# First four key strips by rows of k, the first memory tile alone, and products that nobody reads

## The chip, the core and the metric

One Trainium2 chip, of which this kernel uses one core. The metric is device time in microseconds (us) of one execution. The kernel before takes 1377.06 us, the median of three runs (1375.69 to 1378.71). A core has five engines with a queue of instructions each, worked off in order: TensorE (PE in the profile; its weight loads are PEld), VectorE (DVE), ScalarE (ACT), GpSimd (POOL) and SyncE (SP, which only issues transfers). A wait at the head of a queue holds back all that stands behind it.

## The reference, cut

One layer of an encoder for 256 prompt tokens and 32 sample tokens (288 columns together), width 2048:

```python
h = rmsnorm(x, norm_in)
(a_q, a_k, a_v, i_q, i_k, i_w, a_z, b_z, b_xbc, b_dt, m_q, m_z, gates) = split_cols(h @ w_in)
mkv = rmsnorm(mem_prompt, norm_mem[l]) @ w_mem_kv[l]
mk_p = mkv[..., :M_WIDTH].reshape(bp, N_MEM, M_HEADS, M_HEAD_DIM)
mv_p = mkv[..., M_WIDTH:].reshape(bp, N_MEM, M_HEADS, M_HEAD_DIM)
...
merged = g_a * (ya @ w_pa) + g_b * (yb @ w_pb) + g_m * (ym @ w_pm)
return x + merged @ w_o, (k_new, v_new, i_k, conv_state, h_last)
```

The change is about `mk_p`, the keys of the memory: 256 memory tokens of width 2048, normed, times 2048 x 1024 weights. It is the first thing that the kernel computes.

## The kernel before, in words

All weights (some 200 MB) are streamed once. A weight tile is 512 KB: for a product with 2048 inputs it holds half a strip, that is 128 output channels and 8 of the 16 rows of k (a row of k is 128 inputs). Every weight tile goes through `convert`: SP loads it into `wr`, ACT makes `wh` (a rounded copy in the fast float format), DVE makes `wl` (the rest, `wr - wh`), and PE multiplies. The moving operand is split likewise into a high and a low part, so a row of k is three products: wh with high, wh with low, wl with high. `wr`, `wh` and `wl` have three buffers each.

`jobs` holds the tiles in their order. `run` pops one, calls `convert` for a later one, emits the products (`go`) and then calls `step`, which hands out one piece of side work from the generators that are active, at most two at a time. A generator that yields n comes back n tiles later. `hook` puts a plain function between two tiles. Two `convert` calls stand ahead of `run`, so the third weight tile is converted in the first round.

At the start (lines 70 to 365) the memory is loaded in four tiles of four rows of k (`memraw`, tag A), which ACT and DVE split into `memh` (B) and `meml` (C), with the gain of the norm multiplied in. The norm's root is only needed afterwards, since it is a factor per token. For it, `mem_squares` squares the memory on POOL, two instructions of two rows each in one step, and DVE adds the squares up in `macc` one step later, with a last fold of the two halves. `mem_rstd` lets PE sum `macc` over the partitions (a product with `ones`) and makes the root; `ev_mk` calls it once, when strip 4 is done, scales the four strips that wait in `mkT` (E), and scales the later ones as they come. `x_norm` is the same for the input x (D): eight loads on POOL's queue, squares on ACT, sums on POOL (`ev`), a product with `ones`, and then the split into xh and xl. It must be done when `begin_x` is reached, after all memory products.

The first three strips of keys take the first halves first and the second halves after them; the other five go half after half; then come two blocks of memory values (`mv_block`, 8 tiles each).

Of the kernel before, what the change touches and what calls it, by code (L numbers as in the profile page):

```python
# [7 lines left out]
F32 = mybir.dt.float32  # L8
# [5 lines left out]
P = 128  # L14
# [9 lines left out]

# column blocks of the combined projection, in the order in which the kernel walks them
N_MQ, N_IQ, N_AK, N_AV, N_AQ, N_MZ, N_XBC, N_G = 8, 8, 2, 2, 8, 8, 24, 16
# [7 lines left out]
def step_kernel(ctx, tc, ins, outs):  # L34
# [32 lines left out]
    def mm(out, lhsT, rhs, start=True, stop=True):  # L67
        PE.matmul(out, lhsT, rhs, start=start, stop=stop)  # L68

    # ------------------------------------------------------------------ loads of the start  # L70
    N = Names()
# [8 lines left out]
    S.preload_act_table_set("natural_log_exp_and_others")  # L80
    nc.sync.dma_start(N.memraw[:, 0:4], ins["memT"][:, 0:4])
    cols = const.tile([P, 272], F32, name="cols")
    S.dma_start(cols, ins["cols"])
    g_mem, g_in, g_ssm, g_fin, d_col = (cols[:, 16 * i:16 * i + 16] for i in range(5))
    cw = cols[:, 80:176].rearrange("p (c i) -> p c i", c=24)
# [6 lines left out]
    G.memset(ones, 1.0)  # L92
    ident = const.tile([P, P], F32, name="ident")
    G.affine_select(ident, ones, pattern=[[1, P]], compare_op=OP.is_equal, fill=0.0, base=0,
                    channel_multiplier=-1)
# [3 lines left out]

    # ------------------------------------------------------------------ norms  # L100
    def rsqrt(v, p, n, size):
        """v = 1/sqrt(p / size + EPS), [128, n]; p in PSUM."""
        r, u = t2(n), t2(n)
        S.activation(r, p, AF.Ln, scale=1.0 / size, bias=eps)  # L104
        V.tensor_scalar(v, p, 1.0 / size, EPS, OP.mult, OP.add)
        S.activation(r, r, AF.Exp, scale=-0.5)
        V.scalar_tensor_tensor(u, r, -0.5, r, OP.mult, OP.mult)
        V.tensor_tensor(u, u, v, OP.mult)
        V.scalar_tensor_tensor(v, u, 1.5, r, OP.add, OP.mult)
# [14 lines left out]

    # ------------------------------------------------------------------ the streamed products
    jobs = []          # halves: (dram ap, shape, matmul emitter)
    conv = []          # converted halves that wait for their products
    state = {"c": 0}

    def strip(halves, mov, evac, n=T):  # L130
        """One block of 128 output channels; halves of its weights [128, 8, 128]."""
        box = {}
        for j, ap in enumerate(halves):
            def go(wh, wl, j=j):
                hi, lo = getattr(N, mov) if isinstance(mov, str) else mov
                if j == 0:
                    box["p"] = ps()
                p = box["p"][:, 0:n]
                k0 = 8 * j
                last = j == len(halves) - 1  # L140
                for i in range(8):
                    mm(p, wh[:, i], hi[:, k0 + i], j == 0 and i == 0, False)
                    mm(p, wh[:, i], lo[:, k0 + i], False, False)
                for i in range(8):
                    mm(p, wl[:, i], hi[:, k0 + i], False, last and i == 7)
                if last:
                    evac(p)
            jobs.append((ap, [P, 8, P], go))
# [20 lines left out]
    def hook(f):  # L169
        """f is called between the products before and after it."""  # L170
        jobs.append((None, None, f))

    def convert():
        i = state["c"]
        if i >= len(jobs):
            return
        state["c"] += 1
        ap, shape, go = jobs[i]
        if ap is None:
            conv.append((None, None, go))  # L180
            return convert()
        raw = wpool.tile(shape, F32, tag="wr", name="wr")
        nc.sync.dma_start(raw, ap)
        wh = wpool.tile(shape, F32R, tag="wh", name="wh")
        wl = wpool.tile(shape, F32R, tag="wl", name="wl")
        S.activation(wh, raw, AF.Copy)  # L186
        V.tensor_tensor(wl, raw, wh.bitcast(F32), OP.subtract)  # L187
        conv.append((wh, wl, go))

    # ------------------------------------------------------------------ side work  # L190
    queue, active = [], []
# [8 lines left out]
    def turn(key, gap):  # L200
        """Waits until gap halves have passed since the turn before this one."""
        while clock["t"] < clock.get(key, 0):
# [4 lines left out]
    def later(*fs):  # L207
        """Each of fs one half further on than the one before it."""
        chains.append(list(fs))
# [44 lines left out]

    # ------------------------------------------------------------------ memory keys and values
    N.mkT = slot("E", [P, 8, 256])
# [3 lines left out]

    def mem_load(k0):
        nc.sync.dma_start(N.memraw[:, k0:k0 + 4], ins["memT"][:, k0:k0 + 4])

    def mem_split(k0):
        for k in range(k0, k0 + 4):
            g = g_mem[:, k:k + 1]
# [3 lines left out]

    def mem_squares():
        N.macc = t2()
        sq = []
# [22 lines left out]
    def ev_mk(s):  # L296
        def f(p):
            if s < 4:
                S.activation(N.mkT[:, s], p, AF.Copy)
                return  # L300
            if s == 4:
                mem_rstd()
                V.tensor_tensor(N.mkT[:, 0:4], N.mkT[:, 0:4],
                                N.mr[:, None, 0:256].to_broadcast([P, 4, 256]), OP.mult)
                G.dma_start(outs["mem_k"][:, 0:4], N.mkT[:, 0:4])
            V.tensor_tensor(N.mkT[:, s], p, N.mr[:, 0:256], OP.mult)
            if s == 7:
                G.dma_start(outs["mem_k"][:, 4:8], N.mkT[:, 4:8])
        return f

    def ev_mv(c):
# [5 lines left out]

    def x_norm():
        acc = ev()
        for k in range(0, 16, 2):  # L320
# [22 lines left out]

    for s in range(3):
        strip([ins["w_mk"][s, h] for h in range(2)], (N.memh, N.meml), ev_mk(s), 256)
    jobs[:] = jobs[0::2] + jobs[1::2]
    jobs.insert(1, (None, None, lambda: mem_split(12)))
    for s in range(3, 8):
        strip([ins["w_mk"][s, h] for h in range(2)], (N.memh, N.meml), ev_mk(s), 256)
    for c in range(2):  # L350
        mv_block(c, ev_mv(c))

    mem_split(0)
    convert()
    mem_load(4)
    mem_split(4)
    convert()
    mem_load(8)
    mem_load(12)
    mem_split(8)  # L360
    dts = const.tile([P, 64], F32, name="dts")
# [4 lines left out]

    # ------------------------------------------------------------------ projections of the step
    wi = {"s": 0}
# [40 lines left out]

    # ---- memory attention  # L410

    def softmax(p, c, width_, scale):
        """Rows of p [128, c * width_]: c softmaxes; the maximum is subtracted."""
        m = st()
# [74 lines left out]

    # ---- index keys, index weights, step sizes  # L490
    wt = const.tile([P, 3, 64], F32, name="wt")
# [13 lines left out]

    # columns of dts: step sizes, their products with -exp(a_log), running sums
    dt = const.tile([P, 96], F32, name="dt")
# [5 lines left out]
    def g_misc():  # L513
# [13 lines left out]
        mark("misc")  # L527
        # log(1 + exp(u)) = max(u, 0) + 2 atanh(e / (2 + e)), e = exp(-|u|)
        V.scalar_tensor_tensor(e, u, -1.0, u, OP.mult, OP.max)
# [40 lines left out]

    # ---- index scores
    def begin_a():
# [5 lines left out]
    def score(j):  # L578
        yield from need("misc")
        # a pair of heads, each in its own half of the rows of the array  # L580
        ps_ = [sd(), sd()]
# [104 lines left out]

    # ---- memory branch output
    def ev_mz(j, p):
# [12 lines left out]

    # ------------------------------------------------------------------ convolution, attention
    ASC = 128 ** -0.5
# [69 lines left out]
    cso = const.tile([P, 24, 6], F32, name="cso")  # L773
    # strips: the first group's channels, B, C, the other groups' channels
    order = list(range(4)) + list(range(16, 24)) + list(range(4, 16))
# [32 lines left out]

    # ------------------------------------------------------------------ memory gate; the scan
    def begin_scan():  # L810
# [14 lines left out]
    def scan(g):  # L825
# [28 lines left out]
        yield  # L854
        # x, token-major, times the step size
        px = []
# [16 lines left out]

        # decays from s to t
        def decay(*rs):
# [37 lines left out]
        yield 2  # L913
        # outputs
        po = []
# [53 lines left out]

    # ------------------------------------------------------------------ attention output  # L970
    def ev_az(j, p):
# [8 lines left out]

    # ------------------------------------------------------------------ scan output
    def begin_y():
# [76 lines left out]

    # ------------------------------------------------------------------ output product, last norm  # L1060
    POOLED = (2, 6, 9, 12, 14)
# [134 lines left out]
```

## Time and profile before

| what | us |
|---|---|
| median of three runs | 1377.06 |
| span of the profiled execution, first to last instruction | 1374.1 |
| PE busy | 1347.9 |
| DVE busy | 770.0 |
| ACT busy | 606.4 |
| POOL busy | 237.5 |

The page gives the busy time of each engine, then the chain of work that ended last: it is followed back from the last instruction to whatever released it. Other views answer for a stretch of time: instructions in order of time (start, duration, engine, line, operation, output<-input, shape, count, and in brackets the idle time before and its releaser), groups of them, waits, and the transfers by queue (packets, MB, and the time that they took as a share of 16 transfer engines; q1 is SP's queue, q0 POOL's, q10 ACT's).

This is how the first 40 us stand by engine: length of the stretch, then the busy time and the number of instructions of each, the granted clock of PE, and share and GB/s of the transfers.

```profile
0.00:5.00 5.00, 0.00 (x0) 0.00 (x0) 0.06 (x1) 1.28 (x1) 1.62 (x8) 1.00 0.63 168
5.00:10.00 5.00, 0.71 (x3) 0.71 (x4) 3.28 (x5) 3.26 (x7) 3.72 (x5) 1.00 1.01 297
10.00:15.00 5.00, 3.97 (x14) 2.79 (x13) 5.00 (x5) 3.77 (x9) 4.99 (x6) 1.00 1.03 415
15.00:20.00 5.00, 4.73 (x28) 4.73 (x29) 5.00 (x8) 3.60 (x6) 2.17 (x3) 1.00 1.02 373
20.00:25.00 5.00, 5.00 (x44) 5.00 (x44) 4.97 (x8) 2.12 (x2) 1.68 (x1) 1.00 0.75 273
```

PE's count of products in 5 us rises to 44 only in the last of these rows.

### The profile page before, as it was taken

How to read it: one execution, taken by the hardware profiler on the slowest of the kernel's cores; microseconds unless marked ns; L12 is line 12 of the kernel's file. 1: busy time of each engine (PE TensorE's matmuls, PEld its weight loads, DVE VectorE, ACT ScalarE, POOL GpSimd, SP SyncE). 2: the span in 40 equal slices, each digit the busy share in tenths (PEclk: the TensorE clock that was granted, in tenths of full speed). 3: DMA queues.
4: the chain of work that ended last, by engine and by line, in shares of the span. 5: the costliest groups of instructions: out<-in, count | busy, mean ns of one | idle time of the engine just before them, and what ended most of it. 6: DMA issues, size and time to landing. Idle time of an engine off the chain costs nothing.

```text
span 1374.1 us, 24380 instructions
## 1 busy us (share of the span) xinstructions
PE 1347.9 (98%) x10032; PEld 1315.0 (96%) x10032; DVE 770.0 (56%) x1166; ACT 606.4 (44%) x858; POOL 237.5 (17%) x319
## 2 busy tenths in 40 slices
PE   6999999999999999999999999999999999999995
PEld 6989999899999999999999999999999999999995
DVE  7674344594567766646556556663344334555444
ACT  5654343444555543725425336663333433334331
POOL 5501000000000001122231233410044000000433
PEclk9999999999999999999999999999999999999998
DMA  8667434344444445654545445445456555455552
GB/s 288 212 217 255 143 130 132 118 162 158 165 139 151 151 156 164 224 181 146 179 136 186 165 156 167 159 164 172 166 170 218 173 169 166 157 169 169 170 169 84
DMA packets 63006, 232.03 MB, mean 169 GB/s; under 512 B 7264, under 2 KB 7808, under 8 KB 61744
## 3 DMA queue, kind: packets, MB, share of 16 engines
q1 hardware_dynamic: 57888, 209.72, 46.2%
q0 software_dynamic: 4144, 19.30, 4.3%
q8 instruction: 78, 1.28, 0.4%
q10 hardware_dynamic: 864, 1.47, 0.3%
q14 instruction: 32, 0.26, 0.1%
HBM read 223.06 MB, written 7.33 MB: 168 GB/s over the span
## 4 chain that ended last, share of the span: by engine, by line
PE 98%; DVE 1%; DMA 1%; ACT 0%; issue 0%; DVEq 0%; SPq 0%; ACTq 0%
PE ps L68 91%; PE sd L68 6%; DMA A<-in_memT 1%; DVE A L1089 0%; PE sd L861 0%; DVE C L268 0%; PE sd L727 0%; PE sd L845 0%; PE sd L440 0%; DVEq L1174 0%; ACT B L267 0%; ACT F L314 0%; PE sd L671 0%; ACT t L104 0%; ACT t L590 0%
## 5 line engine op out<-in xcount | busy, mean ns | idle before, releaser
L187 DVE TENSOR_TENSOR wl<-wr,wh 128x1024 fp32r<-128x1024 f32 x394 | 493.4, 1257 | 392.0 <-ACT wh L186 391.2
L68 PE MATMUL ps<-xh,wh 128*128 128x288 f32 x2128 | 582.2, 299 | 0.0
L68 PE MATMUL ps<-xl,wh 128*128 128x288 f32 x2128 | 574.5, 296 | 0.0
L186 ACT ACTIVATE wh<-wr 128x1024 fp32r<-128x1024 f32 x394 | 411.9, 1054 | 239.4 <-PE ps L68 194.8
L68 PEld LDWEIGHTS ps<-xh,wh 128*128 128x128 f32 x2128 | 400.3, 188 | 7.1 <-issue 3.4
L68 PEld LDWEIGHTS ps<-xl,wh 128*128 128x128 f32 x2128 | 400.6, 188 | 1.3 <-issue 0.7
L68 PE MATMUL ps<-xh,wl 128*128 128x288 f32 x2128 | 324.5, 294 | 0.0
L68 PEld LDWEIGHTS ps<-xh,wl 128*128 128x128 f32 x2128 | 296.6, 188 | 0.0
L68 PE MATMUL ps<-B,wh 128*128 128x288 f32 (+1 forms) x384 | 102.9, 296 | 9.3 <-ACT wh L186 9.3
L68 PEld LDWEIGHTS ps<-B,wh 128*128 128x128 f32 x384 | 74.2, 193 | 9.3 <-ACT wh L186 9.3
L68 PE MATMUL ps<-E,wh 128*128 128x288 f32 x256 | 70.2, 302 | 0.0
L68 PE MATMUL ps<-F,wh 128*128 128x288 f32 x256 | 69.5, 296 | 0.0
L68 PE MATMUL ps<-A,wh 128*128 128x288 f32 x256 | 69.2, 299 | 0.0
L68 PE MATMUL ps<-mgl,wh 128*128 128x288 f32 x256 | 69.1, 296 | 0.0
L68 PE MATMUL ps<-mgh,wh 128*128 128x288 f32 x256 | 69.0, 295 | 0.0
L790 POOL COPY cso<-t 128x3 f32<-128x3 f32 x24 | 5.0, 210 | 256.9 <-ACT t L788 256.9
L68 PEld LDWEIGHTS ps<-E,wh 128*128 128x128 f32 x256 | 48.3, 189 | 1.0 <-issue 0.8
L68 PEld LDWEIGHTS ps<-F,wh 128*128 128x128 f32 x256 | 48.1, 188 | 0.2 <-issue 0.2
L68 PEld LDWEIGHTS ps<-A,wh 128*128 128x128 f32 x256 | 48.3, 189 | 0.0
L68 PEld LDWEIGHTS ps<-mgl,wh 128*128 128x128 f32 x256 | 48.2, 188 | 0.0
L68 PEld LDWEIGHTS ps<-mgh,wh 128*128 128x128 f32 x256 | 48.1, 188 | 0.0
L68 PE MATMUL ps<-A,wl 128*128 128x288 f32 x256 | 39.3, 296 | 0.0
(290 smaller groups left out, 1348.5 us busy)
## 6 DMA issues: line engine op xcount, KB each, us to landing
wr<-in_w_in SPq DMA_DIRECT2D x266, 512.0 KB, 3.4
wr<-in_w_pb SPq DMA_DIRECT2D x32, 512.0 KB, 3.7
wr<-in_w_o SPq DMA_DIRECT2D x32, 512.0 KB, 3.3
wr<-in_w_mk SPq DMA_DIRECT2D x16, 512.0 KB, 3.8
wr<-in_w_mv SPq DMA_DIRECT2D x16, 512.0 KB, 4.3
wr<-in_w_pm SPq DMA_DIRECT2D x16, 512.0 KB, 3.3
wr<-in_w_pa SPq DMA_DIRECT2D x16, 512.0 KB, 3.3
B<-scr POOLq DMA_DIRECT2D x4, 1152.0 KB, 9.4
```

Source lines behind the costliest of these rows:

```text
L68: PE.matmul(out, lhsT, rhs, start=start, stop=stop)
L186: S.activation(wh, raw, AF.Copy)
L187: V.tensor_tensor(wl, raw, wh.bitcast(F32), OP.subtract)
L790: G.tensor_copy(cso[:, c, 0:3], u[:, 256:259])
```

## The change

1. **Rows of k in four accumulators.** The first four strips no longer go strip by strip. `mk_rows` takes one row of k (four times) or two (six times) of all four strips at once, into four accumulators that stay open till the last row. A weight tile is then 4 strips x nk rows x 128 columns, in runs of 512 B (one row) or 1 KB (two rows) in memory, instead of 4 KB.
2. **Loads.** Memory row 0 is loaded alone, then row 1, then three pairs, all on SP; rows 8 to 15 go to POOL's queue. Only the gain of the memory's norm (`g_mem`, 8 KB) is loaded first; the rest of `cols` follows after three conversions.
3. **Unused products.** PE multiplies `ones` with itself eight times at the start.
4. **Side work.** `mem_squares` begins with `yield 9`, `x_norm` with `yield 3`. `mem_rstd` is called at strip 6 instead of strip 4. Memory rows are split as jobs of their own (`"now"`), in `convert`.
5. Three `convert` calls of weight tiles stand ahead of `run`.

```diff
-    nc.sync.dma_start(N.memraw[:, 0:4], ins["memT"][:, 0:4])
+    g_mem = const.tile([P, 16], F32, name="g_mem")
+    S.dma_start(g_mem, ins["cols"][:, 0:16])
+    nc.sync.dma_start(N.memraw[:, 0:1], ins["memT"][:, 0:1])
     cols = const.tile([P, 272], F32, name="cols")
-    S.dma_start(cols, ins["cols"])
...
+    warm = sd()
+    for _ in range(8):
+        mm(warm[:, 0:P], ones, ones)
...
         if ap is None:
-            conv.append((None, None, go))
+            if shape == "now":
+                go()
+            else:
+                conv.append((None, None, go))
             return convert()
...
     def mem_squares():
+        yield 9
         N.macc = t2()
...
-            if s < 4:
+            if s < 6:
                 S.activation(N.mkT[:, s], p, AF.Copy)
                 return
-            if s == 4:
+            if s == 6:
                 mem_rstd()
-                V.tensor_tensor(N.mkT[:, 0:4], N.mkT[:, 0:4],
-                                N.mr[:, None, 0:256].to_broadcast([P, 4, 256]), OP.mult)
-                G.dma_start(outs["mem_k"][:, 0:4], N.mkT[:, 0:4])
+                for a in (0, 3):
+                    V.tensor_tensor(N.mkT[:, a:a + 3], N.mkT[:, a:a + 3],
+                                    N.mr[:, None, 0:256].to_broadcast([P, 3, 256]), OP.mult)
             V.tensor_tensor(N.mkT[:, s], p, N.mr[:, 0:256], OP.mult)
             if s == 7:
-                G.dma_start(outs["mem_k"][:, 4:8], N.mkT[:, 4:8])
+                G.dma_start(outs["mem_k"], N.mkT)
...
+    def mk_rows(k0, nk, box):
+
+        def go(wh, wl):
+            if k0 == 0:
+                box["p"] = [sd()[:, 0:256] for _ in range(4)]
+            for n, (w, m) in enumerate(((wh, N.memh), (wh, N.meml), (wl, N.memh))):
+                for s in range(4):
+                    for i in range(nk):
+                        mm(box["p"][s], w[:, s, i], m[:, k0 + i], k0 == 0 and n == 0 and i == 0,
+                           k0 + nk == 16 and n == 2 and i == nk - 1)
+            if k0 + nk == 16:
+                for s in range(4):
+                    ev_mk(s)(box["p"][s])
+        a = ins["w_mk"][0:4, k0 // 8, :, k0 % 8:k0 % 8 + nk].rearrange("s p k c -> p s k c")
+        jobs.append((a, [P, 4, nk, P], go))
...
     def x_norm():
+        yield 3
         acc = ev()
...
+    ROWS = ((0, 1), (1, 1), (2, 1), (3, 1), (4, 2), (6, 2), (8, 2), (10, 2), (12, 2), (14, 2))
+    box = {}
+    for k0, nk in ROWS:
+        if k0 >= 3:
+            jobs.append((None, "now", lambda k0=k0, nk=nk: mem_split(k0, nk)))
+        mk_rows(k0, nk, box)
+    for s in range(4, 8):
         strip([ins["w_mk"][s, h] for h in range(2)], (N.memh, N.meml), ev_mk(s), 256)
...
-    mem_split(0)
+    mem_split(0, 1)
     convert()
-    mem_load(4)
-    mem_split(4)
+    mem_load(1, 1)
+    mem_split(1, 1)
     convert()
-    mem_load(8)
-    mem_load(12)
-    mem_split(8)
+    mem_load(2, 2)
+    mem_split(2, 1)
+    convert()
+    S.dma_start(cols[:, 16:272], ins["cols"][:, 16:272])
+    for k in (4, 6):
+        mem_load(k, 2)
+    for k in (8, 12):
+        mem_load(k, 4, G)
```

The order of the built program shows what this does to POOL's queue, from its first work on: before (`A` is the memory, `D` is x, `t` the squares, `ev` the squares of x and their sum).

```order
L92 MEMSET ones 128x128
L94 AFFINE_SELECT ident<-ones 128x128
L97 AFFINE_SELECT tri<-ones 128x128
L363 DMA dts<-in_dts 128x64
L277 TENSOR_TENSOR t_183<-A 128x512
L277 TENSOR_TENSOR t_185<-A 128x512
L321 DMA D<-in_xT 128x576 x2
L277 TENSOR_TENSOR t_230<-A 128x512
L277 TENSOR_TENSOR t_232<-A 128x512
```

And now, on the same engine from the same place.

```order
L270 DMA A<-in_memT 128x1024 x2
L396 DMA dts<-in_dts 128x64
L347 DMA D<-in_xT 128x576 x8
L355 TENSOR_TENSOR ev<-ev 128x288 x2
L286 TENSOR_TENSOR t_456<-A 128x512
L286 TENSOR_TENSOR t_458<-A 128x512
L355 TENSOR_TENSOR ev<-ev 128x288 x3
L286 TENSOR_TENSOR t_501<-A 128x512
L286 TENSOR_TENSOR t_503<-A 128x512
L355 TENSOR_TENSOR ev<-ev 128x288 x3
L286 TENSOR_TENSOR t_547<-A 128x512
L286 TENSOR_TENSOR t_549<-A 128x512
```

All loads of x moved ahead of the first compute, two loads of memory came in, and the squares of memory moved in between the sums of x. On VectorE the last sums of the squares stood among the conversions (`wl`) of the sixth, seventh and eighth weight tile before:

```order
L187 TENSOR_TENSOR wl<-wr,wh 128x1024
L283 TENSOR_TENSOR t_183<-t_183,t_269 128x512
L283 TENSOR_TENSOR t_183<-t_183,t_271 128x512
L187 TENSOR_TENSOR wl<-wr,wh 128x1024
L283 TENSOR_TENSOR t_183<-t_183,t_308 128x512
L283 TENSOR_TENSOR t_183<-t_183,t_310 128x512
L285 TENSOR_TENSOR t_183<-t_183 128x256
L187 TENSOR_TENSOR wl<-wr,wh 128x1024 x5
L105 TENSOR_SCALAR mr<-sd 128x258
```

Now the same stretch, which ends in the first instruction of the memory's root (`mr`) and begins with the sixteenth weight tile, reads:

```order
L195 TENSOR_TENSOR wl<-wr,wh 128x1024
L292 TENSOR_TENSOR t_456<-t_456,t_547 128x512
L292 TENSOR_TENSOR t_456<-t_456,t_549 128x512
L195 TENSOR_TENSOR wl<-wr,wh 128x1024
L292 TENSOR_TENSOR t_456<-t_456,t_593 128x512
L292 TENSOR_TENSOR t_456<-t_456,t_595 128x512
L294 TENSOR_TENSOR t_456<-t_456 128x256
L195 TENSOR_TENSOR wl<-wr,wh 128x1024 x2
L110 TENSOR_SCALAR mr<-sd 128x258
```

Between the fold (L285, now L294) and the root there were five conversions and are now two.

More of the change, by code (lines that the diff above doesn't have):

```diff
@@ L80, in step_kernel @@
     S.preload_act_table_set("natural_log_exp_and_others")
-    nc.sync.dma_start(N.memraw[:, 0:4], ins["memT"][:, 0:4])
+    g_mem = const.tile([P, 16], F32, name="g_mem")
+    S.dma_start(g_mem, ins["cols"][:, 0:16])
+    nc.sync.dma_start(N.memraw[:, 0:1], ins["memT"][:, 0:1])
     cols = const.tile([P, 272], F32, name="cols")
-    S.dma_start(cols, ins["cols"])
-    g_mem, g_in, g_ssm, g_fin, d_col = (cols[:, 16 * i:16 * i + 16] for i in range(5))
+    g_in, g_ssm, g_fin, d_col = (cols[:, 16 * i:16 * i + 16] for i in range(1, 5))
     cw = cols[:, 80:176].rearrange("p (c i) -> p c i", c=24)
@@ L259, in step_kernel, with mem_load, mem_split @@
     N.xr = evp.tile([P, T], F32, tag="ya", bufs=2, name="xr")
[L261 to L265, printed above, removed]
+    def mem_load(k0, n, eng=None):
+        (eng or nc.sync).dma_start(N.memraw[:, k0:k0 + n], ins["memT"][:, k0:k0 + n])
+    def mem_split(k0, n):
+        for k in range(k0, k0 + n):
             g = g_mem[:, k:k + 1]
@@ L342, in x_norm @@
         mark("x")
[L344 to L348, printed above, removed]
+    ROWS = ((0, 1), (1, 1), (2, 1), (3, 1), (4, 2), (6, 2), (8, 2), (10, 2), (12, 2), (14, 2))
[5 more added lines that the diff above has]
+    for s in range(4, 8):
         strip([ins["w_mk"][s, h] for h in range(2)], (N.memh, N.meml), ev_mk(s), 256)
```

## The prediction

> **What bounds the kernel now.** I began with the page: the busy times of its first part, then the chain that ended last.
>
> ```profile
> PE 1347.9 (98%) x10032; PEld 1315.0 (96%) x10032; DVE 770.0 (56%) x1166; ACT 606.4 (44%) x858; POOL 237.5 (17%) x319
> ```
>
> TensorE is the bound: 1374.1 us of span less 1347.9 busy leaves 26 us. A change that neither removes nor speeds up products can win only where PE waits. So the next view is the list of PE's waits, and then the chain over the first 60 us.
>
> ```profile
> PE ps L68 <- ACT wh L186: 9.3, 1, 9.3
> PE ps L68 <- DVE C L268: 1.2, 3, 0.4
> PE sd L68 <- DVE ev L1080: 0.6, 1, 0.6
> PE sd L68 <- ACT t L590: 0.5, 1, 0.5
> ```
>
> ```profile
> 1.71 7.76 DMA A<-in_memT
> ...
> 12.78 2.44 DVE C L268 x2
> 15.23 0.04 issue
> 15.27 28.61 PE ps L68 x225
> 43.87 0.77 PE sd L68 x6
> ```
>
> Up to 9.3 us PE waits for the loads, until 15.3 for the splits of the memory tiles on VectorE; from there it is full. The timeline of PE shows one thing more.
>
> ```profile
> 17.36 0.41 PE L68 MATMUL ps<-B,wh 128*128 128x256 f32 x1
> 17.57 0.41 PE L68 MATMUL ps<-C,wh 128*128 128x256 f32 x1
> ...
> 20.68 0.28 PE L68 MATMUL ps<-B,wh 128*128 128x256 f32 x1
> 20.80 0.28 PE L68 MATMUL ps<-C,wh 128*128 128x256 f32 x1
> ...
> 23.55 0.28 PE L68 MATMUL ps<-B,wh 128*128 128x256 f32 x1
> ...
> 43.71 0.59 PE L68 MATMUL sd<-t,ones 128*128 128x256 f32 x2
> ```
>
> Starts are 0.21 us apart at 17.4 (the slow rate after an idle stretch) and 0.12 at 20.7. One half strip of 24 products takes 23.55 - 20.68 = 2.87 us. The product of the memory norm starts at 43.71, after ten halves, so the first four strips (eight halves) end at 43.71 - 2 x 2.87 = **38.0 us**. Most that the head can give: first product at about 5.5 us, 192 products of 0.12 and 24 of them slow (0.09 more each) end at 30.8, which is 7.2 us earlier.
>
> **The change: the head.** Four strips by rows of k need 128 KB of memory and 256 KB of weights for 12 products, where a half strip needed 512 KB of each. The first product comes earlier. By the rate of the first slices below, 0.39 MB (memory tile 0 and weight tile 0) have moved by 3.5 us; with some 1.5 us to land (0.54 MB had moved by 4.0, and POOL could read the first memory tile at 5.58, in a row further down) and half of a conversion, PE starts at about 5.5 instead of 9.3. But all eight loads of x and the second half of memory now stand in POOL's queue ahead of any compute; before, each pair of x loads followed a pair of squares. What matters is how two queues share the 16 DMA engines. These are the GB/s of 1 us slices from 0 to 40, then rows of queues in five windows: 3 to 4, 5 to 6, 6 to 7, 16 to 18 and 116 to 118 us.
>
> ```profile
> GB/s 0 53 189 295 304 387 156 107 422 414 418 432 422 396 406 410 401 382 355 316 381 328 213 106 336 193 307 123 78 281 398 381 258 242 29 221 274 82 328 188
> ```
> ```profile
> q10 hardware_dynamic: 53, 0.06, 20.2%
> ```
> ```profile
> q0 software_dynamic: 2, 0.00, 25.4%
> ```
> ```profile
> q0 software_dynamic: 14, 0.03, 114.8%
> ```
> ```profile
> q0 software_dynamic: 165, 0.63, 84.2%
> ```
> ```profile
> q0 software_dynamic: 71, 0.54, 64.7%
> q1 hardware_dynamic: 74, 0.29, 35.5%
> ```
>
> The last two rows carry the argument: 71 packets of POOL's queue (q0) against 74 of SP's (q1), yet 0.54 MB against 0.29. The queues take turns packet by packet, whatever a packet's size. After the change SP's packets are 512 B (a run of one strip and one row), POOL's stay at 4 KB and more. Prices: an x load (288 KB) costs 2 x 0.842 / 0.63 x 0.295 = 0.79 us, four packets per engine; 512 KB of memory at the 0.41 MB/us of the slices 1.3 us, eight packets; dts 0.25 + 1.15 = 1.4 us, first seen in the slice at 5 us, though its issue began at 1.57:
>
> ```profile
> 1.57 0.74 POOL L363 DMA_DIRECT2D dts<-in_dts  x1
> ```
>
> POOL's queue therefore starts near 5.8 and holds 2 x 1.3 + 1.4 + 8 x 0.79 = 10.3 us, 49 packets per engine. A 512 B packet isn't in the trace: q10's 53 packets of 1.1 KB took 0.202 x 16 / 53 = 61 ns each, so it lies between half of that by size and all of it; I take 40 ns, nearer the half. In turn with 49 of POOL's packets SP gets 49 of its own: the last 10 of weight tile 1, 8 of memory 2-3, 31 of the 32 of weight tile 2, some 2.3 us. Weight tile 2 is across at 5.8 + 10.3 + 2.3 = 18.4 and landed at 19.4; PE, done with two rows by 12, starts the third at 20.0 at the slow rate (12 x 0.21 = 2.6) and, with tile 3 behind memory 4-7, the fifth row at 25.4. The other 12 rows are 12 x 12 x 0.12 = 17.2 us: the four strips end at 42.6 instead of 38.0, **+4.6 us**. Bounds: -7.2 (PE's own pace) and +7 (512 B at the price of 1.1 KB: 0.021 us more on some 115 packets per engine, 2.4).
>
> **The memory norm.** Squares of memory are put off by nine halves, those of x by three, so both now meet on POOL, in turn: 2 adds, 2 squares, 3 adds, 2 squares, and so on, 11 adds and 8 squares before the last square. VectorE's sums wait for them, and PE's norm product, now after strip 6 instead of strip 4, waits for the sums with everything behind it. Rows of ACT, POOL and DVE, then two grouped ones (0 to 60 us, and 39 to 41):
>
> ```profile
> 32.68 1.10 ACT L327 ACTIVATE ev<-D 128x288 f32<-128x288 f32 x3
> 33.68 1.05 ACT L186 ACTIVATE wh<-wr 128x1024 fp32r<-128x1024 f32 x1
> ```
> ```profile
> 5.58 2.21 POOL L277 TENSOR_TENSOR t<-A 128x512 f32<-128x512 f32 x2 [3.27 <-DMA A<-in_memT]
> ```
> ```profile
> 23.32 4.00 POOL L277 TENSOR_TENSOR t<-A 128x512 f32<-128x512 f32 x2 [6.15 <-DVE t L283]
> ...
> 33.53 13.38 POOL L329 TENSOR_TENSOR ev<-ev 128x288 f32<-128x288 f32 x11 [5.15 <-ACT ev L327]
> ```
> ```profile
> 30.85 1.48 DVE L283 TENSOR_TENSOR t<-t,t 128x512 f32<-128x512 f32 x2
> 32.37 0.42 DVE L285 TENSOR_TENSOR t<-t 128x256 f32<-128x256 f32 x1
> ```
> ```profile
> L277 POOL TENSOR_TENSOR t<-A 128x512 f32<-128x512 f32 x8 | 11.7, 1480 | 10.1 <-DVE t L283 6.1 <-DMA A<-in_memT 4.0
> ```
> ```profile
> L329 POOL TENSOR_TENSOR ev<-ev 128x288 f32<-128x288 f32 x3 | 2.4, 810 | 0.2
> ```
>
> Let T be the end of the ninth weight tile (rows 12 and 13). ACT's twelfth conversion (1.05) is released there, the first squares of x follow, and POOL starts 33.53 - 32.68 = 0.85 later: T + 1.9. Then 13.4 for 11 adds, 11.7 for 8 squares, 1.5 + 0.4 for the last sums and the fold: **T + 28.9**. PE has one row tile and six halves until then, 7 x 2.87 = 20.1. Wait: **+8.8 us**. Bounds: adds at 0.81 and squares at 1.10 give 1.4; squares at 2.0 (beside VectorE's sums, as they will be) give 13. After some 9 idle us the first 24 products run at 0.21: 24 x 0.09, **+2.0** (0 to 2.7). POOL's four last adds and the x norm hide behind strip 7.
>
> **The rest.** Three weight tiles instead of two are converted ahead of the loop, so each step's side work stands one conversion later on ACT and VectorE. PE's only such wait now is 0.5; I add **+0.5** (0 to 3). The eight unused products can start when ones is set:
>
> ```profile
> 0.80 0.20 POOL L92 MEMSET ones<- 128x128 f32 x1 [0.29 <-POOLq L1166]
> ```
> ```profile
> 44.14 0.50 PE L68 MATMUL sd<-ones,t 128*128 128x1 f32 x4
> ```
>
> The f32 product of 256 columns took 44.14 - 43.71 = 0.43, so one of 128 at half the rate takes as much, and eight are done by 4.5, in idle time (nothing; 1 us if they took the double). The split load of cols (136 KB) takes its place in the same load time, the scaling of six keys in two parts is VectorE work in cover of strip 7, and one store less is POOL's: nothing each, at most 0.5 either way.
>
> Sum: 4.6 + 8.8 + 2.0 + 0.5 = 15.9; the span goes from 1374.1 to 1390.0. Around the span the median of 1377.06 has 3.0 more: **1393.0 us**.
>
> **Rivals.** A, shares by bytes: SP gets half, 0.2 MB/us from 5.8 on. Then the third tile is in at 9, the fifth at 15.3, rows run from 17.4 and end at 34.6, -3.4 instead of +4.6: 1385.0. For it: nothing in the rows; against it, 71 and 74. The Trainium skill, DMA: Bandwidth & Descriptors, section Queues, rings and completion order, says that an engine drains a whole packet of some 9 to 17 descriptors before it switches; if SP's 512 B pieces went so bundled, A would come out. The rows of q10, where pieces of 1.1 KB are counted singly, speak against it.
> C, the loads don't collide at all (POOL's issue comes late): -7.2 for the head, the norm's wait stays: 1374.1 - 7.2 + 11.3 + 3.0 = 1381.2.
> B, faster: POOL keeps up. Its chain takes its quickest rows, the wait is 1.4 and PE stays at its rate; it decides at 20.1 us for the chain. With the head at its best: 1374.1 - 7.2 + 1.4 + 0.5 + 3.0 = 1371.8. For it: 0.81 and 1.10 occur; against it: never while VectorE works.
> D, the rows aren't early at all, because landing, not size, sets the start: PE begins at 9.3, rows three and four still wait for the same tile, and the time is the forecast's.
>
> **Chances.** Forecast 0.60 with D 0.05, A 0.18, C 0.08, B 0.09. The likeliest is 1393.0. The range: down to C (1382), and up to two thirds of the way to all upper bounds at once (7 + 13 + 2.7 + 3 makes 1402.8): 1399. About 0.2% (2.8 us) can be told from no change: slower 0.88, within 0.05, faster 0.07.
>
> **What would show it.** Head: weight tile 2 landing near 19, PE idle from 12 to 20; if it lands by 12, A or C holds. Norm: PE's longest wait before the product of ones, ended by VectorE's fold, 6 to 12 us; POOL busy without a gap for 25 us before it. Slow rate after both gaps. Afterwards the same spacing as before, to 1 us. Wrong would make it a POOL that works beside VectorE undisturbed, or packets bundled for SP.

## The result, and the profile after

The changed kernel takes **1397.24 us** (median of four runs, 1394.86 to 1398.56), the kernel before 1376.58 beside it: a ratio of 1.0147 (95% interval 1.0135 to 1.0159), 20.7 us slower. The forecast was 1393.0, range 1382 to 1399.

The profiled executions are 22.8 us apart by their spans, 1396.9 against 1374.1. That is 2.1 more than the medians, in part since the profiled execution of after is the slowest of its four runs, with a span 1.4 above the middle of theirs. Around its span the changed kernel has 1.7 to 1.8 us in all four runs, the kernel before 2.0 or more wherever span and time are on record together; the forecast added 3.0 and so has 1.3 too much there. From the page of the changed kernel, first part, and then its list of what PE waits for (us in total, times, longest):

```profile
PE 1362.6 (98%) x10048; PEld 1328.6 (95%) x10048; DVE 766.6 (55%) x1167; ACT 621.9 (45%) x862; POOL 227.9 (16%) x320
```
```profile
PE sd L68 <- DVE t L294: 8.1, 1, 8.1
PE sd L68 <- ACT wh L194: 8.0, 3, 4.2
PE ps L68 <- ACT wh L194: 0.7, 1, 0.7
```

The longest wait is the forecast one, on the fold of the memory's squares (L294). But PE is also busy for 14.7 us more, with 16 passes more that took 3.8: some products ran slower. PE's timeline tells where: the second and the third row of k, the last two rows, the first product behind the rows, the norm's product, that of x, the first product of the values.

```profile
12.97 1.22 PE L68 MATMUL sd<-B,wh 128*128 128x256 f32 x4 [4.16 <-ACT wh L194]
...
18.65 0.74 PE L68 MATMUL sd<-B,wh 128*128 128x256 f32 x4 [2.75 <-ACT wh L194]
...
37.72 1.12 PE L68 MATMUL sd<-B,wh 128*128 128x256 f32 x8
...
40.60 0.28 PE L68 MATMUL ps<-B,wh 128*128 128x256 f32 x1
...
67.13 1.19 PE L68 MATMUL sd<-t,ones 128*128 128x256 f32 x2 [8.09 <-DVE t L294]
...
74.09 0.68 PE L68 MATMUL sd<-ev,ones 128*128 128x288 f32 x2
...
77.47 0.40 PE L68 MATMUL ps<-wh,B 128*128 128x512 f32 x1
```

The rows end at 40.60 instead of 38.0 (+2.6). The values begin at 77.47 instead of 62.33, **+15.1**: 2.6 of the head, 8.1 + 0.7 of waits, and 3.2 of products at the slow rate (from 67.13 to 74.09 are 6.96 us, for which one half strip and the norm's products took 3.75 before, from 43.71 to 47.46); the 0.5 left over goes mostly where PE stops and starts again. POOL and then VectorE show the chain behind the wait:

```profile
39.37 2.06 POOL L355 TENSOR_TENSOR ev<-ev 128x288 f32<-128x288 f32 x2 [27.36 <-ACT ev L353]
41.39 3.02 POOL L286 TENSOR_TENSOR t<-A 128x512 f32<-128x512 f32 x2
...
60.54 2.03 POOL L286 TENSOR_TENSOR t<-A 128x512 f32<-128x512 f32 x2
```
```profile
63.58 2.48 DVE L292 TENSOR_TENSOR t<-t,t 128x512 f32<-128x512 f32 x2
66.09 0.90 DVE L294 TENSOR_TENSOR t<-t 128x256 f32<-128x256 f32 x1
```

The other 7.7 us of the 22.8 come later, where the change has edited nothing. A part of them is in the chain that ended last: eight weight tiles of x width in one piece (192 products), first in the kernel before, then in the changed one.

```profile
878.73 25.50 PE ps L68 x192
```
```profile
900.27 25.56 PE ps L68 x192
```

That is 3.187 and 3.195 us a tile; from the start of one dense tile to the next the traces have 3.187 and 3.200. Nothing waits there. This was in none of the forecast's terms, and four of the runs below are about it.

### The profile page after: what moved, and what is told of

Same layout as the page of the kernel before. It is cut to its first block, busy times and chain, and to the rows that moved or that the text cites. A ratio compares the mean times of both kernels' runs of the same rounds, so it can differ in the third digit from the quotient of the medians.

```text
span 1396.9 us, 24430 instructions
## 1 busy us (share of the span) xinstructions
PE 1362.6 (98%) x10048; PEld 1328.6 (95%) x10048; DVE 766.6 (55%) x1167; ACT 621.9 (45%) x862; POOL 227.9 (16%) x320
## 4 chain that ended last, share of the span: by engine, by line
PE 91%; DVE 1%; ACT 0%; issue 0%; DVEq 0%; ACTq 0%
PE ps L68 85%; PE sd L68 6%; DVE A L1122 0%; PE sd L894 0%; PE sd L760 0%; ACT t L623 0%; ACT wh L194 0%; PE sd L878 0%; PE sd L473 0%; DVEq L1207 0%; PE sd L704 0%; ACT t L109 0%; DVE ev L1113 0%; DVE t L113 0%; DVE A L1106 0%
## 5 line engine op out<-in xcount | busy, mean ns | idle before, releaser
L195 DVE TENSOR_TENSOR wl<-wr,wh 128x1024 fp32r<-128x1024 f32 (+1 forms) x396 | 489.3, 1237 | 586.9 <-ACT wh L194 586.3
L194 ACT ACTIVATE wh<-wr 128x1024 fp32r<-128x1024 f32 (+1 forms) x396 | 416.8, 1054 | 640.7 <-PE ps L68 507.1
L68 PE MATMUL ps<-B,wh 128*128 128x288 f32 (+1 forms) x320 | 86.8, 297 | 0.7 <-ACT wh L194 0.7
L823 POOL COPY cso<-t 128x3 f32<-128x3 f32 x24 | 23.0, 959 | 242.1 <-ACT t L821 242.1
L68 PEld LDWEIGHTS ps<-B,wh 128*128 128x128 f32 x320 | 61.4, 192 | 1.0 <-ACT wh L194 1.0
L68 PE MATMUL ps<-A,wl 128*128 128x288 f32 x256 | 39.4, 296 | 0.0
```

The lines of the kernel that those rows point to most:

```text
L823: G.tensor_copy(cso[:, c, 0:3], u[:, 256:259])
```

## Experiments

What each run reached, in us: the start of the third row of k, the end of the four strips, the first product of the values, the first of x, and the median.

| run | third row | strips end | values | x | median |
|---|---|---|---|---|---|
| before | | 38.0 | 62.3 | 106.3 | 1376.6 |
| after | 18.65 | 40.6 | 77.5 | 121.7 | 1397.2 |
| sums of x late | 18.4 | 40.7 | 64.6 | 113.4 | 1392.8 |
| loads first | 18.55 | 44.0 | 68.3 | 113.6 | 1388.7 |
| squares first | 12.1 | 39.4 | 63.8 | 108.8 | 1385.0 |
| half strips, late norm | | 40.8 | 72.4 | 116.4 | 1385.9 |
| before, 64 B further | | 38.0 | 62.4 | 106.3 | 1381.4 |
| no unused products | 18.2 | 40.3 | 77.4 | 121.6 | 1396.5 |
| x in sixteen loads | 15.6 | 41.8 | 77.6 | 121.9 | 1400.2 |
| all mended | 14.7 | 39.4 | 63.7 | 108.7 | 1378.5 |
| after, 64 B further | 18.9 | 41.6 | 76.9 | 121.2 | 1392.6 |
| before, 128 B further | | 38.0 | 62.7 | 106.7 | 1373.6 |
| two ahead | 20.7 | 42.5 | 73.6 | 117.5 | 1390.8 |
| in one queue | 9.0 | 33.9 | 59.7 | 104.3 | 1373.3 |

### Sums of x late: do the two chains meet on POOL?

```diff
-        yield
+        yield 6
         for k in range(16):
             q = acc if k == 0 else ev()
```

> The changed kernel, but the sums of x begin five steps later, behind the last squares of the memory; the eight loads of x stay where they are, ahead of all compute on POOL. Theory (the two chains meet on POOL): POOL then has 8 squares between the ninth weight tile and the fold, T + 1.9 + 11.7 + 1.9 = T + 15.5, under the 20.1 us of work that PE has left. PE's wait before the product of ones goes from 8.1 to 0, the slow products of strip 7 (2.4 us) go with it, and the memory values begin 10 to 11 us earlier, near 67 instead of 77.5. The head stays: rows end near 40.6. The root of x is now later, so up to 8 us may come back where the values end and x must be split; the whole lies between 1386 and 1395. Rival (squares put off are too late by themselves, meeting or not): the wait stays above 5 us and the values begin after 74.

Measured: 1392.77 (ratio 1.0119, 1.0104 to 1.0134), the values at 64.64. From the timeline of POOL of this run:

```profile
11.86 1.05 POOL L286 TENSOR_TENSOR t<-A 128x512 f32<-128x512 f32 x1
14.98 1.04 POOL L286 TENSOR_TENSOR t<-A 128x512 f32<-128x512 f32 x1 [2.07 <-DMA A<-in_memT]
18.47 5.34 POOL L286 TENSOR_TENSOR t<-A 128x512 f32<-128x512 f32 x4 [2.45 <-DMA A<-in_memT]
46.17 1.04 POOL L286 TENSOR_TENSOR t<-A 128x512 f32<-128x512 f32 x1 [22.36 <-DVE t L292]
48.97 1.04 POOL L286 TENSOR_TENSOR t<-A 128x512 f32<-128x512 f32 x1 [1.76 <-DVE t L292]
```

The wait is gone: the values begin 12.8 us earlier with the same head. The theory's sum was too cautious: with no sum of x ahead of them in the queue, six of the eight squares run as soon as the memory has landed, without regard to the step in which they are issued. So it was the position **behind a blocked add** that delayed them, not the `yield 9` itself. Of the 12.8, 8.4 are left when x begins. The first tile of the values takes 6.58 us instead of 2.75, as PE now waits there for VectorE's scaling of the keys and runs slowly behind that wait:

```profile
67.34 0.50 PE L68 MATMUL ps<-wh,B 128*128 128x512 f32 x1 [2.07 <-DVE E L315]
```

At the end 6.0 are left by the spans (4.5 by the medians), since the norm of x is now late: PE waits four times for the split of x (`xl`), 1.0 us in all, and the products between those waits run slowly.

### Loads first, squares first: what holds the third row?

Both start the squares of the memory at the first step. In the first, the eight loads of x stay ahead in POOL's queue (they are issued in one go ahead of `side`, and `x_norm` begins with `yield 5` in their place); in the second they come behind the squares, and its whole edit is this:

```diff
     def mem_squares():
-        yield 9
         N.macc = t2()
```

> The changed kernel, but the squares of the memory start at the first step instead of the tenth; the eight loads of x stay ahead of all compute in POOL's queue. Theory: the norm's wait (8.1 and 2.4 of slow products) goes; the third row of k still waits for its weight tile behind POOL's queue and starts near 18.7. New cost: the splits of memory rows 8 to 15 on VectorE now run beside squares on POOL, 0 to 4 us in the rows. The whole: 1397.2 - 11 + (0 to 4) = 1386 to 1390. Rival (the head is not slowed by the loads of x but by something that the early squares remove): third row before 15 and the whole under 1383.

> As the run before, but the loads of x stand behind the eight squares in POOL's queue, and so start when the memory has landed. Theory (POOL's queue starves SP's 512 B pieces): without 32 packets of x per engine ahead, the third weight tile lands 4 to 6 us earlier, the third row starts near 13, and the rows end up to 5.7 us before those of the run with the loads first; the whole 1381 to 1386. Rival A (SP gets its share by bytes, x doesn't matter): third row still near 18, difference to the run with the loads first under 1 us.

Measured: 1388.71 (1.0092, 1.0077 to 1.0107) and 1385.03 (1.0066, 1.0049 to 1.0083). The third row in PE's timeline, first with the loads first, then with the squares first:

```profile
18.55 1.22 PE L68 MATMUL sd<-B,wh 128*128 128x256 f32 x4 [3.62 <-ACT wh L194]
```
```profile
12.11 1.12 PE L68 MATMUL sd<-B,wh 128*128 128x256 f32 x4
```

The loads of x are what delays the third row, by 6.4 us; rival A (x doesn't matter) is out. At the end of the rows 4.6 of it are left, in the time 3.7. Both runs lose in the rows what the early squares cost: a pair of memory splits on VectorE, alone in the changed kernel and beside POOL's squares in the run with the loads first:

```profile
21.48 0.87 DVE L276 SCALAR_TENSOR_TENSOR C<-A,g_mem,B 128x256 fp32r<-128x256 f32 x2
```
```profile
21.77 2.44 DVE L276 SCALAR_TENSOR_TENSOR C<-A,g_mem,B 128x256 fp32r<-128x256 f32 x2
```

### Half strips with the late norm: are the rows of k to blame?

The kernel before, with the side work of the change alone.

```diff
     def mem_squares():
+        yield 7
...
     def x_norm():
+        yield 1
...
-            if s == 4:
+            if s == 6:
                 mem_rstd()
```

> The kernel before, with its half strips, memory tiles and loads, and of the change only the side work: squares of the memory and of x put off so that the fold stands as far ahead of the product of ones as in the changed kernel (two steps less, since the four strips take two tiles less), the root at strip 6, scaling in two parts, one store. Theory: the wait comes without the rows too: PE waits 6 to 10 us before the product of ones, slow products 2, the whole 1384 to 1389. Rival (the rows of k make POOL or PE late): no wait, 1376 to 1378.

Measured: 1385.94 (1.0071, 1.0056 to 1.0086), values at 72.4 instead of 62.3. The 6 to 10 us of waiting were expected right before the product of ones; 4.5 came, and further ahead, on a conversion of ACT. The two waits on PE, then ACT just before the second of them:

```profile
53.95 0.39 PE L68 MATMUL ps<-B,wh 128*128 128x256 f32 x1 [1.46 <-ACT wh L186]
...
60.10 0.39 PE L68 MATMUL ps<-B,wh 128*128 128x256 f32 x1 [3.02 <-ACT wh L186]
```
```profile
58.66 0.44 ACT L329 ACTIVATE ev<-D 128x288 f32<-128x288 f32 x1 [0.76 <-POOL ev L331]
59.01 1.04 ACT L186 ACTIVATE wh<-wr 128x1024 fp32r<-128x1024 f32 x1
```

ACT's squares of x wait for a buffer that POOL frees, and the conversion stands behind them: the same full POOL, reaching PE by another door. So 9.7 of the 20.7 us need no rows. The strips, too, end 2.8 us later than before, with x's loads in front and 4 KB pieces on SP: the head's loss is not one of small pieces alone.

### Before, 64 bytes further: why is a weight tile slower?

```diff
+    pad = const.tile([P, 16], F32, name="pad")
     cols = const.tile([P, 272], F32, name="cols")
```

> The kernel before, with 64 bytes per partition reserved ahead of cols and never used, so that every buffer behind it, the weight tiles among them, lies 64 bytes further, as it does in the changed kernel (where the gain of the memory's norm takes those 64 bytes). In the traces a weight tile of x (24 products, dense) takes 3.187 us in the kernel before and with half strips and the late norm, and 3.200 in the changed kernel and the three other runs with rows of k. Theory (place of the weight tiles): 3.200 here too, and the whole 3 to 5 us slower, 1379 to 1381. Rival (the order or the number of PE's instructions): 3.187, and the whole within 1 us of 1376.5.

Measured: 1381.38 (1.0034, 1.0021 to 1.0046), 4.9 us slower by a buffer that nobody uses. The chain:

```profile
883.10 25.56 PE ps L68 x192
```

The place of the buffers it is. Compared product by product with the kernel before, PE loses some 4.0 us steadily and 1.5 in one place near 238 us, of which the last section tells.

### No unused products

```diff
-    warm = sd()
-    for _ in range(8):
-        mm(warm[:, 0:P], ones, ones)
```

> The changed kernel without the eight unused products of PE at the start. Theory: they stand in idle time and cost nothing; the third row waits for its weight tile as before, the norm's wait follows from the ninth: 1396 to 1398. A weight tile of x stays at 3.200 us (place of the tiles) where the rival of the run above says that PE's instructions set it, 3.187 and 1393. Second rival (they warm PE's clock): without them the first rows run at the slow rate longer and the rows end 1 to 2 us later.

Measured: 1396.50 (1.0145, 1.0131 to 1.0159). The values begin at 77.4, the tile stays at 3.200. They cost nothing and bring nothing that the times show.

### x in sixteen loads

```diff
-            G.dma_start(N.x[:, k:k + 2], ins["xT"][:, k:k + 2])
+            for j in (k, k + 1):
+                G.dma_start(N.x[:, j:j + 1], ins["xT"][:, j:j + 1])
```

> The changed kernel, with x loaded one row of k at a time: sixteen loads of 144 KB instead of eight of 288 KB, so that the pieces on POOL's queue are half as long, with the same bytes. Theory (the queues take turns by pieces): in the time of x's load SP gets up to twice its pieces; the third weight tile lands 2 to 4 us earlier, the third row starts at 15 to 17 instead of 18.65, and the memory values begin as much earlier, at 73.5 to 76 instead of 77.5; the whole 1393 to 1396. Rival A (shares by bytes): third row within 0.7 us of 18.65, the whole 1396 to 1398. If the pieces turn out as long as before, the run tells nothing of this.

Measured: 1400.18 (1.0166, 1.0152 to 1.0180). The third row came at 15.64, the fourth at 20.42; the values stayed at 77.6. The queues of 10 to 12 us and of 12 to 14 us:

```profile
q0 software_dynamic: 180, 0.53, 71.1%
q1 hardware_dynamic: 371, 0.21, 35.4%
```
```profile
q1 hardware_dynamic: 503, 0.59, 87.3%
q0 software_dynamic: 43, 0.12, 18.4%
```

A piece of POOL's queue had 2.9 KB (0.53 MB / 180) instead of 3.7, far from half; and the third tile got through when POOL's queue ran nearly dry from 12 to 14. So this run doesn't decide between turns and bytes, and its 1400.18 lies above the ranges of both. In its profiled execution the slow stretch near 252 us (last section) costs 1.5 us more than in that of the changed kernel. It does show that a row gained at the third tile is lost at the fourth as long as x is still under way.

### All mended

Squares from the first step, one per step; loads of x behind them, then `dts`; root at strip 5; 64 bytes more behind `g_mem`.

> Rows of k with the losses taken away that the runs have shown: squares of the memory from the first step, one per step, each added up a step later; loads of x behind the squares, and the broadcast of dts behind those; the root at strip 5, scaling in one part; and 64 bytes more reserved, so that the weight tiles lie as the kernel before has them modulo 128 bytes. Theory: the run with the squares first (1385.0), less 4 by the place of the weight tiles, less 2 to 5 in the rows, where VectorE no longer waits for two squares at once: 1376 to 1379, about the kernel before. Rival (the place of the tiles is not it): 1380 to 1383.

Measured: 1378.51 (1.0013, 1.0004 to 1.0022). The rows still wait twice for weight tiles: for the second one, while POOL's queue has nothing but rows 8 to 15 of the memory, and for a later one when the loads of x have been under way:

```profile
12.00 1.22 PE L68 MATMUL sd<-B,wh 128*128 128x256 f32 x4 [5.00 <-ACT wh L194]
...
30.53 1.22 PE L68 MATMUL sd<-B,wh 128*128 128x256 f32 x8 [2.34 <-ACT wh L194]
```

### After, 64 bytes further; before, 128 bytes further

```diff
-    g_mem = const.tile([P, 16], F32, name="g_mem")
+    g_mem = const.tile([P, 32], F32, name="g_mem")
```

> The changed kernel with 64 more bytes per partition reserved behind the gain of the memory's norm, and nothing else: the weight tiles then lie as in the run with all mended, where one takes 3.180 us. Theory: the head and the norm's wait stay (values near 77.5), some 340 tiles of x width lose 0.02 us each, 6 to 7 us: 1390 to 1393. Rival (the 64 bytes matter only with half strips): 1396 to 1398.

> The kernel before with 128 bytes per partition reserved ahead of cols (the run before reserved 64 and lost 4.9 us). Theory: the weight tiles lie as in the run with all mended, 3.180 us each instead of 3.187: 2 to 3 us faster than the kernel before, 1373.5 to 1375. Rival (what counts is only the place modulo 128, and the rest came from the rows): 3.187 and 1376 to 1377.

Measured: 1392.58 (1.0118, 1.0102 to 1.0133) and 1373.58 (0.9978, 0.9969 to 0.9987). In the chain of either kernel, the changed and the one before, eight tiles take:

```profile
893.92 25.43 PE ps L68 x192
```
```profile
877.69 25.43 PE ps L68 x192
```

That is 3.179 us a tile; from start to start the dense tiles take 3.173 and 3.180, about as often the one as the other. One place gives 3.187 us a tile, 64 bytes further 3.200, 128 further 3.176 on average, the same in both kernels. In the changed kernel the move brings 4.7 us; in the kernel before, 3.2.

### Two conversions ahead

```diff
     mem_split(2, 1)
-    convert()
```

> The changed kernel with two conversions of weight tiles ahead of the loop instead of three. The prediction gave the third +0.5 us. Theory now: the third conversion puts the squares of x behind a conversion that waits for the ninth weight tile, and with two it waits for the eighth; POOL's chain then begins 2.9 us earlier and the norm's wait falls from 8.1 to about 5; the whole 1393 to 1395.5. Rival (the +0.5 of the prediction): the wait stays at 8, the whole 1396 to 1397.

Measured: 1390.79 (1.0102, 1.0089 to 1.0116), values 3.9 us earlier though the rows end 1.9 later. PE's waits from the end of the rows to the norm's product add up to 4.5 us instead of 8.8:

```profile
55.17 0.39 PE L68 MATMUL ps<-B,wh 128*128 128x256 f32 x1 [1.03 <-ACT wh L194]
...
61.31 0.39 PE L68 MATMUL ps<-B,wh 128*128 128x256 f32 x1 [3.01 <-ACT wh L194]
...
66.42 0.67 PE L68 MATMUL sd<-t,ones 128*128 128x256 f32 x2 [0.48 <-DVE t L294]
```

The third conversion put the squares of x, and with them POOL's chain, one tile later. That is a term of the norm's wait, not of "the rest". But the whole fell below the 1393 that were expected, and the difference lies behind the values. By the spans this run leads the changed kernel by 7.5, of which the most is found: 3.9 at the values, 0.3 in the values, where a wait of 0.4 on ACT is gone, 1.4 between 271 and 279 us, in small products of the attention (`sd<-C,B`, 64 rows), and 1.5 by a slow stretch that this execution doesn't have (last section). At the first of those products (0.7 of the 1.4) a copy of VectorE (L599), for which PE idles 0.48 us, stands behind a conversion in the changed kernel and ahead of it here; 6 us on it is ACT's reading of the products (L623) that stands behind one. VectorE in the changed kernel, then in this run:

```profile
271.23 1.23 DVE L195 TENSOR_TENSOR wl<-wr,wh 128x1024 fp32r<-128x1024 f32 x1 [2.06 <-ACT wh L194]
...
272.47 0.43 DVE L599 COPY t<-sd 32x288 f32<-32x288 f32 x1
```
```profile
265.79 0.43 DVE L598 COPY t<-sd 32x288 f32<-32x288 f32 x1
...
267.47 1.21 DVE L195 TENSOR_TENSOR wl<-wr,wh 128x1024 fp32r<-128x1024 f32 x1
```

All runs with three conversions ahead lose this 1.4, and none of those with two does (this one and the four with half strips).

### In one queue

The run with all mended, but memory rows and x are loaded on SP, each ahead of its weight tile, and the root is taken at strip 7.

```diff
-            G.dma_start(N.x[:, k:k + 2], ins["xT"][:, k:k + 2])
+            nc.sync.dma_start(N.x[:, k:k + 2], ins["xT"][:, k:k + 2])
...
+            def now(k0=k0, nk=nk):
+                if k0 in (3, 4, 6):
+                    mem_load(*{3: (4, 2), 4: (6, 2), 6: (8, 2)}[k0])
+                elif k0 in (8, 10, 12):
+                    mem_load(k0 + 2, 2)
+                mem_split(k0, nk)
```

> The run with all mended, but the loads of x and the memory rows from 4 on stand on SP's own queue, each ahead of the weight tile that comes with it, so that no other queue takes turns with the weight tiles while the rows run; the root at strip 7. Theory (turns by pieces): in one queue a load costs its bytes alone (0.7 us for a pair of rows of x), the second row starts before 9 instead of 12.0, the rows end at 34 to 37 instead of 39.4, the values begin at 59 to 62 instead of 63.7; the whole 1373 to 1377, at or below the kernel before. Rival (the memory's bytes are the limit, whatever the queue): rows end at 39 or later, the whole 1378 to 1381.

Measured: **1373.32** (0.9979, 0.9970 to 0.9988), faster than both kernels. PE's timeline: third row, end of the rows.

```profile
9.04 0.74 PE L68 MATMUL sd<-B,wh 128*128 128x256 f32 x4
...
33.86 0.29 PE L68 MATMUL ps<-B,wh 128*128 128x256 f32 x1
```

The rows end 4.1 us before the half strips of the kernel before and 6.7 before the changed kernel. But the kernel before gets as far with 128 unused bytes, 1373.58, so the rows have no advantage that the times show. Against that run they lead by 3.1 us at the values and 2.4 at x; in the profiled executions 1.5 us go in a slow stretch near 236 us (last section) and 1.4 between 253 and 261 us, in the small products that pay for the third conversion ahead, which this run still has. Loads in one queue with two conversions ahead weren't run.

## Why the prediction was right, and where it wasn't

**The norm's wait** was right in mechanism and size: T + 28.9 was forecast for the fold, and with T at 37.7 (the last two rows begin) it ended at 66.99, T + 29.3. PE's own work from there took 20.1 and a wait of 0.7; 8.1 was left. That it fits so closely is luck, as errors in the terms cancelled: 11 adds took 14.4 instead of 13.4 and eight squares 9.1 instead of 11.7, while VectorE's last sums and fold took 3.4 instead of 1.9, beside POOL, and stood another 1.0 behind a conversion. Taking away the meeting brought the values 12.8 us earlier, and putting it into the kernel before made that one slower by 9.7 (2.8 of it in the strips).

**The slow rate** after the wait was there: the granted clock of 65 to 70 us is 0.50 (time, PE busy, clock, share and GB/s of the transfers).

```profile
65.00:70.00 5.00, 2.87 (x11) 0.50 0.33 119
```

The Trainium skill, TensorE: Matmul & The Clock Gate, Part 1, has the clock halved after an idle window of some 3.4 us; with 8.1 us of waiting the trace agrees. The half strip behind the wait took 5.26 us instead of the 2.95 of the same one before, 2.3 more where 2.0 was forecast, and the norm's products 0.9 more, for which the forecast has no term.

**The head** had the right sign and mechanism; the term was too large, +2.6 instead of +4.6. PE didn't idle in one piece from 12 to 20: it waited 4.16 for the tile of the second row, which started at 12.97 where I had both rows done by 12, and 2.75 for that of the third. The third row started at 18.65 (forecast 20.0), and the fourth and fifth followed without the further wait that I had put in. The turns of two queues, from 10 to 12 us of the changed kernel:

```profile
q0 software_dynamic: 175, 0.64, 84.1%
q1 hardware_dynamic: 174, 0.13, 20.5%
```

175 pieces against 174, 0.64 MB against 0.13: turn by turn, as argued from 71 and 74. It was nearly so from 12 to 14 us too (172 against 190). From 6 to 8 us, though, POOL had 119 and SP 330, and from 14 to 16 it was 125 against 288; whether a queue had run dry on some of the engines there isn't shown, so the turns are shown for some stretches and not as a rule. The Trainium skill, DMA: Bandwidth & Descriptors, section Queues, rings and completion order, lets an engine drain 9 to 17 descriptors before it switches; the counts of a window can't tell single pieces from bundles of like number, here or in the rows of q10. Rival A with its fair share by bytes is refuted for these windows, C by the waits for the second and third row, D by a first product at 5.88 instead of 9.3, and B by POOL's adds: they took 1.0 to 1.4 us each instead of 0.81, though three of the four pairs of squares kept the quick pace (1.02 each).

**The third conversion ahead** was right as a mechanism, side work one conversion later, but mis-sized: +0.5 was forecast (0 to 3), and 0.3 in the values and 1.4 in the small products of the attention came. Taking it back brought 6.4 by the medians, since 3.9 more stand ahead of the values. Those were in the sum under another name, as the choice of T (the ninth weight tile and not the eighth), so the forecast was no worse for them; but it would have named the wrong culprit. **The unused products** cost nothing, as said, and no wait of PE in the changed kernel ends on the split load of cols or on the scaling of the keys. The scaling was in cover only because the norm's wait came first: with the sums of x late PE waits 2.07 us for it.

**What was missing** are the 7.7 us that come after the values have begun. Of these, 4.0 are the place of the buffers (64 bytes of `g_mem` ahead of them), as the kernel before showed with 64 bytes more. About 1.5 are a slow stretch near 252 us, 0.3 and 1.4 are the third conversion's, and 0.5 is spread out. "Afterwards the same spacing as before, to 1 us" was thus wrong. That the forecast is only 4.2 under the result is luck in part: 2.0 too much for the head and 1.3 too much around the span stood against what was missing.

## What to carry to other kernels

Side work that is put off lands on whatever else was put off: list, per engine, what else is released in the same steps, and count the chain from the first instruction that blocks the queue, not from the step that issues it. A prefetch on a second queue is not free while the first one is needed: with the loads in one queue, in the order of need, the rows ended 5.5 us earlier here (33.9 against 39.4; queue and order were changed together). Converting one tile further ahead is not free either, as it puts all side work behind it. And after an edit that adds a small buffer, compare the time of one unedited steady tile before anything else is explained.

## What the runs showed of the hardware

**The place of the operands counts.** Everything allocated behind 64 more bytes per partition moved, the weight tiles among them, and each tile of 24 products of 288 columns went from 3.187 to 3.200 us; 128 bytes further it took 3.173 or 3.180. The middle one of all dense tiles is the same to the nanosecond in every run of one place. Which of the moved buffers does it, and by what, wasn't separated.

**The granted clock can drop without a wait of PE.** After 32 narrow products (128x32) that kept PE busy, it fell to half for 3.4 us in the changed kernel; in the kernel before, at the same products, it stayed. Windows of 2 us right behind them, changed kernel first:

```profile
252.00:254.00 2.00, 2.00 (x9) 0.50 0.54 156
```
```profile
236.00:238.00 2.00, 2.00 (x17) 1.00 0.77 250
```

It did so in 8 of the 14 profiled executions, whatever they had changed, so it isn't put down to the change. The Trainium skill, TensorE: Matmul & The Clock Gate, Part 1, gives idle time as the reason for the slow clock; here the profile shows none ahead of the drop. What decides it wasn't found.
